# A hybrid backbone block: score products and gate broadcasts over 128 rows instead of 64

## The chip, the core and the metric

The kernel runs as one program on one core of a Trainium2 chip. The metric is the device time of an execution, in microseconds (us). The engines are named as the profile names them: PE (TensorE, matrix products; its weight loads are shown as PEld), DVE (VectorE), ACT (ScalarE), POOL (GpSimd) and SP (SyncE, which here only issues transfers). PE's work is a stream of pairs, a weight load and a product; a product takes a stationary operand of up to 128 rows by 128 columns and streams the columns of a moving operand past it. The profile writes the shape of the array that a product uses as rows*columns: 128*128, or 64*128 where the operands have 64 rows.

## The reference

Two layers work on 256 latent and 256 context tokens of 1024 features; every layer is a feed-forward, a mixer and a second feed-forward. The change touches only the mixer of the first (even) layer, which runs two kinds of heads side by side, four of each:

```python
# differential attention: two score maps of 64 features a head
s = einsum('bqhcd,bkhcd->bhcqk', q, k) * 64 ** -0.5
p = softmax(s)
w = p[:, :, 0] - lam * p[:, :, 1]
out = einsum('bhqk,bkhe->bqhe', w, v)
...
# mLSTM, both directions; 64 features in queries and keys, 128 in values
bcum = cumsum(lf)
dmat = where(tril, bcum[t] - bcum[s] + ig[s], -inf)
s = einsum('bhtd,bhsd->bhts', qc, kc) * exp(dmat - m_t)
h = (einsum('bhts,bhse->bhte', s, vc) + ...) / max(abs(den), exp(-m_t))
...
y = concat([rms_norm(attn), rms_norm(mem) * sigmoid(o_pre)]) @ w_out
```

Context queries see the 256 context keys, latent queries all 512.

## The kernel before

All streams are kept with features on partitions. For precision every float32 operand of a product is split into a high and a low part (float32r), and a product of two such operands is three products: high·high, high·low and low·high (lines 146 to 148 for the projections, 632 to 634 where tokens are on partitions). Weights are loaded raw by SP into a ring of three tiles; ACT casts the high part (line 120), DVE makes the low part (line 121).

The even mixer (`even_mixer`) starts with the projections of the mLSTM queries and keys (`mq`), then the gates: DVE computes cumulative sums and running maxima, and `ga`, 64 rows that hold the gate values of both directions, is split into `gah` (ACT) and `gal` (DVE). `decay_exps(h)` needs one row of `ga`, with all tokens, on all 128 partitions: a product with a one-hot column of `oneh` as the stationary operand, broadcast to 128 columns, does that, once over `gah` (line 799) and once over `gal` (line 800), for both directions of each mLSTM head.

`stack` prepares the score operands of a pair of halves A (partitions 0 to 63) and B (64 to 127), the features of two mLSTM heads or of the two maps of an attention head. For each half there is a 128-row tile of queries, [high, low], and one of keys, [high, high]; the low parts of the keys of both halves share one tile `kl`, half A's in its upper rows and half B's in its lower ones. The tuple `e` says which engine does each of the five steps; the last, the keys' low part (line 843), is POOL's in all six stacks. `score` (lines 849 and 850) then makes a 128-query block of scores of two products into one PSUM bank: the 128-row one, and one of queries' high parts with keys' low parts over the 64 rows of the half. A head has three units: both context blocks (256 keys each), then each latent block (512 keys). So an mLSTM head makes two pairs of products with 256 columns and two with 512, and an attention head (two maps) four and four: 24 pairs of each width in all.

After the scores of a unit come ACT's exponentials, DVE's sums, normalization and combination of two maps or directions (lines 865 to 878, 954 to 970), PE's transposes of the weights (line 890), ACT's copy out (line 892), the products with the values (line 903), the rms norm of the output (`rms_rows`, line 909) and the transposes back (line 912). Between them stand the big projections `ps_v` and `ps_fm`, which fill PE while the other engines work: `qk_pair` (queries and keys of two attention heads, copied out by ACT on line 933 into `qk`), `rows_pair`, `opre_pair`, and the output projection `ps_y`.

The order on each engine is set by a scheduler over the whole program; waits and buffers come from tiles: a tile of a pool has a tag, and tiles of the same tag share its slots, the later one waiting until the earlier one's last reader is done. Projections go to two PSUM banks (`mm_bank`), mLSTM heads to three (`bank_m`), attention heads to three (`bank_a`). The eight `qk` tiles have buffers of their own and are made ahead of the attention; the tiles of a stack are taken from slots of other tiles that are free by then (`slots1`), as the lists at the calls of `stack` and `stack_a` say.

Of the kernel before, what the change touches and what calls it, by code (L numbers as in the profile page):

```python
# [17 lines left out]
P = 128  # L18
# [16 lines left out]
def backbone_kernel(  # L35
# [96 lines left out]
    def split_spare(r3, m, new):  # L132
        """the same into four tiles of half the rows each, where a phase has room for them"""
# [100 lines left out]
    def gemm_first(tiles, bank):  # L234
        """first output tiles of a phase: the norm of the latents between the products of the context"""
# [44 lines left out]
    def norm_steps(l, n, i, sl, bank):  # L280
        """a norm in steps: the tokens' factors, then each chunk of features"""
# [19 lines left out]
    def out_pass(pairs, streams, units, acts, bank, gate, nxt, between=()):  # L301
        """units: (k0, nk, loader) of the rows that a pair of output tiles needs."""
# [273 lines left out]
            # the vectors that come later  # L576
# [10 lines left out]
            # lam[:, 3]: minus the attention's lambda  # L587
# [20 lines left out]
    def proj_first(w, c0, emits, bank, sbank, spare):  # L608
        """c0: columns of the two pairs of tiles; sbank: for the norm's sums"""
# [32 lines left out]
    def rms_rows(src, n, pool, tag):  # L642
        """[tokens, n heads or blocks, features] -> 1 / rms over the features, in columns"""
# [8 lines left out]
        # one Newton step  # L652
# [6 lines left out]
    def out_weights(w, m0, spares):  # L659
        """four output tiles' weights; spares: new tiles for those that spares names, None for the usual ones"""  # L660
# [19 lines left out]
    def even_mixer(nxt):  # L680
# [31 lines left out]
        # mLSTM queries and keys  # L712
# [228 lines left out]
        def stack_a(h, slots):  # L941
            stacks[h] = stack(qk[h], qk[4 + h], slots1(*slots), (nc.vector.tensor_copy, nc.vector.tensor_copy, nc.scalar.copy, nc.vector, nc.gpsimd))
# [505 lines left out]
```

## Time and profile before

| | us |
|---|---|
| median of 3 runs | 1822.99 |
| lowest and highest | 1822.88 and 1828.3 |
| span of the profiled execution | 1823.0 |
| PE busy in it | 1786.7 (98%) |
| DVE, ACT, POOL busy in it | 1153.7, 737.6, 123.1 |
| mean granted TensorE clock | 0.994 |

The span of the profiled execution is its time from the first to the last instruction; it is the median of the runs within 0.01 us. Of the span some 200 us, from about 457 to 652 us, are the heads of the even mixer. PE's busy time counts the modelled length of every product, and products overlap; how fast PE goes is read from the distance between the starts of successive products.

### The profile page before, as it was taken

Reading aid. Unit: us, or ns where it says so; the run is one execution under the profiler, and the core shown is the slowest. Engines: PE = TensorE matmul, PEld = TensorE weight load, DVE = VectorE, ACT = ScalarE, POOL = GpSimd, SP = SyncE. Lnnn points to the kernel's source line nnn. Section 1 sums busy time; section 2 is a strip of 40 time slices with the busy share of each in tenths; the row PEclk is TensorE's granted clock in tenths of the full one; section 3 lists DMA queues with packets and bytes.
Section 4 is the critical chain, followed back from the end, with each engine's and each line's share of the span. In section 5 each row is a group of like instructions: output and inputs, shape, how many; then the busy total and the mean of one; then the engine's idle time right before and its main releaser. Section 6 shows DMA issues by size and latency. Waiting matters only on the chain.

```text
span 1823.0 us, 24907 instructions
## 1 busy us (share of the span) xinstructions
PE 1786.7 (98%) x10095; PEld 1509.5 (83%) x10095; DVE 1153.7 (63%) x1671; ACT 737.6 (40%) x1274; POOL 123.1 (7%) x174
## 2 busy tenths in 40 slices
PE   7999999998999999999999999999999999999998
PEld 5777778898787789777788898777788998889996
DVE  5767776557657857677753476777552747955555
ACT  4322222245656755222222262222222555654443
POOL 1000000014000102000000020000000200010000
PEclk9999999999999999999999999999999999999999
DMA  9555545543121123455543354555432533236553
GB/s 299 168 184 185 184 161 180 165 136 100 48 70 47 47 93 103 155 179 180 181 167 110 104 179 162 164 183 185 162 127 93 182 109 93 70 102 194 191 196 115
DMA packets 209303, 262.29 MB, mean 144 GB/s; under 512 B 6864, under 2 KB 188663, under 8 KB 209189
## 3 DMA queue, kind: packets, MB, share of 16 engines
q1 hardware_dynamic: 208160, 259.28, 43.6%
q8 instruction: 79, 1.29, 0.3%
q0 software_dynamic: 576, 0.84, 0.2%
q10 hardware_dynamic: 452, 0.59, 0.1%
q14 instruction: 36, 0.29, 0.0%
HBM read 259.64 MB, written 1.05 MB: 143 GB/s over the span
## 4 chain that ended last, share of the span: by engine, by line
PE 87%; DVE 7%; ACT 3%; issue 2%; DMA 1%; POOL 1%; SPq 0%; POOLq 0%; ACTq 0%; DVEq 0%
PE ps_ab L146 16%; PE ps_ab L147 16%; PE ps_ab L148 16%; PE ps_y L146 7%; PE ps_y L148 7%; PE ps_y L147 7%; PE ps_fm L146 2%; PE ps_fm L147 2%; PE ps_fm L148 2%; DVE wlo L121 1%; PE po L903 1%; PE ada_ps L190 1%; PE ps_l L1378 1%; PE ps_l L1379 1%; PE ps_v L632 1%
## 5 line engine op out<-in xcount | busy, mean ns | idle before, releaser
L120 ACT CAST whi<-raw 128x1024 fp32r<-128x1024 f32 (+1 forms) x326 | 335.9, 1031 | 847.4 <-PE ps_ab L147 489.8
L121 DVE TENSOR_TENSOR wlo<-raw,whi 128x1024 fp32r<-128x1024 f32 (+1 forms) x326 | 393.1, 1206 | 317.6 <-ACT whi L120 311.2
L146 PE MATMUL ps_ab<-hh,whi 128*128 128x512 f32 (+1 forms) x1360 | 491.0, 362 | 0.8 <-DVE xT L296 0.7
L147 PE MATMUL ps_ab<-hl,whi 128*128 128x512 f32 (+1 forms) x1360 | 490.1, 361 | 1.6 <-POOL hl L275 1.3
L148 PE MATMUL ps_ab<-hh,wlo 128*128 128x512 f32 (+1 forms) x1360 | 489.1, 360 | 0.3 <-DVE wlo L121 0.3
L178 DVE SCALAR_TENSOR_TENSOR acc<-raw_ada,cs,acc 128x1024 f32<-128x1024 f32 x224 | 276.5, 1281 | 41.0 <-DMA raw_ada<-in_ada_w_dram 41.0
L146 PEld LDWEIGHTS ps_ab<-hh,whi 128*128 128x128 f32 x1360 | 255.3, 188 | 49.0 <-ACT whi L120 5.1
L147 PEld LDWEIGHTS ps_ab<-hl,whi 128*128 128x128 f32 x1360 | 255.7, 188 | 45.2 <-POOL hl L275 1.9
L148 PEld LDWEIGHTS ps_ab<-hh,wlo 128*128 128x128 f32 x1360 | 255.6, 188 | 43.5 <-DVE wlo L121 0.5
L148 PE MATMUL ps_y<-gh,wlo 128*128 128x512 f32 (+1 forms) x660 | 229.9, 348 | 0.4
L146 PE MATMUL ps_y<-gh,whi 128*128 128x512 f32 (+1 forms) x660 | 230.0, 348 | 0.0
L147 PE MATMUL ps_y<-gl,whi 128*128 128x512 f32 (+1 forms) x660 | 228.8, 347 | 0.0
L148 PEld LDWEIGHTS ps_y<-gh,wlo 128*128 128x128 f32 x660 | 124.9, 189 | 17.7 <-DVE wlo L121 1.6
L146 PEld LDWEIGHTS ps_y<-gh,whi 128*128 128x128 f32 x660 | 124.9, 189 | 17.2 <-ACT whi L120 1.2
L349 DVE TENSOR_TENSOR s<-ps_ab,s 128x512 f32<-128x512 f32 (+1 forms) x88 | 54.8, 624 | 131.8 <-PE ps_ab L148 130.7
L147 PEld LDWEIGHTS ps_y<-gl,whi 128*128 128x128 f32 x660 | 124.9, 189 | 15.5
L257 POOL TENSOR_TENSOR ssum<-ssum,sq 128x256 f32<-128x256 f32 x33 | 36.2, 1098 | 1133.8 <-ACT sq L255 1133.0
L146 PE MATMUL ps_fm<-hh,whi 128*128 128x256 f32 (+1 forms) x256 | 85.4, 334 | 0.0
L148 PE MATMUL ps_fm<-hh,wlo 128*128 128x256 f32 (+1 forms) x256 | 85.2, 333 | 0.1
L147 PE MATMUL ps_fm<-hl,whi 128*128 128x256 f32 (+1 forms) x256 | 85.3, 333 | 0.0
L633 PE MATMUL ps_v<-wlo,hh 128*128 128x256 f32 x256 | 74.4, 291 | 3.4 <-DVE wlo L121 3.4
L632 PE MATMUL ps_v<-whi,hh 128*128 128x256 f32 x256 | 74.0, 289 | 0.7 <-ACT mv L636 0.7
(377 smaller groups left out, 2395.1 us busy)
## 6 DMA issues: line engine op xcount, KB each, us to landing
raw<-in_ffn_w_in_dram SPq DMA_DIRECT2D x84, 1024.0 KB, 5.3
raw_ada<-in_ada_w_dram SPq DMA_DIRECT2D x64, 1024.0 KB, 5.0
raw<-in_ffn_w_out_dram SPq DMA_DIRECT2D x41, 1024.0 KB, 5.0
raw<-in_even_w_in_dram SPq DMA_DIRECT2D x12, 1024.0 KB, 5.4
raw<-in_odd_w_in_dram SPq DMA_DIRECT2D x12, 1024.0 KB, 5.5
raw<-in_ffn_w_out_dram SPq DMA_DIRECT2D x15, 768.0 KB, 4.2
raw_c<-in_ada_w_dram SPq DMA_DIRECT2D x16, 512.0 KB, 7.6
raw<-in_even_w_out_dram SPq DMA_DIRECT2D x4, 1024.0 KB, 5.5
```

The source lines that it names most:

```text
L120: nc.scalar.copy(hi3, r3)
L121: eng.tensor_tensor(lo3, r3, hi3.bitcast(F32), ALU.subtract)
L146: nc.tensor.matmul(ps, lhsT=wh, rhs=ah, start=first, stop=False)
L147: nc.tensor.matmul(ps, lhsT=wh, rhs=al, start=False, stop=False)
L148: nc.tensor.matmul(ps, lhsT=wl, rhs=ah, start=False, stop=last)
L178: nc.vector.scalar_tensor_tensor(ada_acc[i], r3[:, k2], s, ada_acc[i], ALU.mult, ALU.add)
L190: nc.tensor.matmul(ps[32 * j : 32 * j + 32, :256], lhsT=unit_e[:, 2 * (n - first) + i], rhs=acc[i][:, j * 256 : j * 256 + 256], start=n == ...
L257: (nc.gpsimd if i else nc.vector).tensor_tensor(ssum[i][0], ssum[i][0], sq, ALU.add)
L349: nc.vector.tensor_tensor(s[:, sl], ps[1][:, sl], s[:, sl], ALU.mult)
L632: nc.tensor.matmul(o, lhsT=ah, rhs=wh[:, k4], start=k == 0 and t % 2 == 0, stop=False)
L633: nc.tensor.matmul(o, lhsT=ah, rhs=wl[:, k4], start=False, stop=False)
L903: nc.tensor.matmul(po[:, t], lhsT=w[:, kt, (t % 2) * P : (t % 2) * P + P], rhs=v[:, kt, h * P : h * P + P], start=kt == 0, stop=kt == nk - 1,)
```

## The change

Two places are changed, and the slots of some tiles with them. The comments are dropped too, and lines move by two or three: line 801 after is 799 and 800 before, 840 is new, 846 is 843, 852 and 853 are 849 and 850.

The gates' low parts go into rows 64 to 127 of the tile whose rows 0 to 63 hold the high parts (`gahl`), and `oneh` has the same one-hot columns in both halves. One product over 128 rows then sums both parts, where there were two over 64 rows.

Each half gets a tile of low parts of its own, `kl0` and `kl1`. Its other 64 rows are set to zero by POOL, and the second score product takes the whole query tile and the whole of that tile, 128 rows: the queries' low parts meet zeros.

```diff
-        gah = mp_.tile([P, TT], F32R, tag="gah", name="gah")[0:H2]
-        gal = mp_.tile([P, TT], F32R, tag="gal", name="gal")[0:H2]
-        oneh = mp_.tile([H2, H2], F32R, name="oneh")
-        nc.vector.tensor_copy(oneh, ident[0:H2, 0:H2])
+        gahl = mp_.tile([P, TT], F32R, tag="gah", name="gahl")
+        gah, gal = gahl[0:H2], gahl[H2:P]
+        oneh = mp_.tile([P, H2], F32R, name="oneh")
+        for r in (slice(0, H2), slice(H2, P)):
+            nc.vector.tensor_copy(oneh[r], ident[r, r])
...
-                sel = oneh[:, 32 * d + h : 32 * d + h + 1].to_broadcast([H2, P])
-                nc.tensor.matmul(pA, lhsT=sel, rhs=gah, start=True, stop=False)
-                nc.tensor.matmul(pA, lhsT=sel, rhs=gal, start=False, stop=True)
+                sel = oneh[:, 32 * d + h : 32 * d + h + 1].to_broadcast([P, P])
+                nc.tensor.matmul(pA, lhsT=sel, rhs=gahl, start=True, stop=True)
...
-            (q0, q1, kk0, kk1, kl) = tl
+            (q0, q1, kk0, kk1, kl0, kl1) = tl
             A, B = slice(0, 64), slice(64, P)
-            for qq, kk, s, o in ((q0, kk0, A, B), (q1, kk1, B, A)):
+            for kl, o in ((kl0, B), (kl1, A)):
+                nc.gpsimd.memset(kl[o].bitcast(F32), 0.0)
+            for qq, kk, kl, s, o in ((q0, kk0, kl0, A, B), (q1, kk1, kl1, B, A)):
...
-            return (q0, kk0, kl, A), (q1, kk1, kl, B)
+            return (q0, kk0, kl0), (q1, kk1, kl1)
...
-            nc.tensor.matmul(ps, lhsT=q[s, tk], rhs=kl[s, :n], start=False, stop=True)
+            nc.tensor.matmul(ps, lhsT=q[:, tk], rhs=kl[:, :n], start=False, stop=True)
...
-        qk = [mp_.tile([P, TT], F32, name=f"qk{t}") for t in range(8)]
+        qk = lazy(lambda t: mp_.tile([P, TT], F32, tag=f"qk{t}", name=f"qk{t}"))
...
-        mstk = [stack(mq[0], mq[2], half2 + slots1(("wTa2", 1)), ...
+        mstk = [stack(mq[0], mq[2], half2 + slots1(("wTa2", 1), ("qk2", 1)), ...
...
-        stack_a(0, (("mq1", 1), ("mq3", 1), ("spare", 1), ("th", 2), ("th", 2)))
+        stack_a(0, (("mq1", 1), ("mq3", 1), ("spare", 1), ("th", 2), ("th", 2), ("qk6", 1)))
...
-        stack_a(1, (("mq0", 1), ("mq2", 1), ("gah", 1), ("gal", 1), ("E02", 1)))
+        stack_a(1, (("mq0", 1), ("mq2", 1), ("gah", 1), ("gal", 1), ("E02", 1), ("qk7", 1)))
...
-        stack_a(2, (("spare", 1), ("E02", 1), ("E03", 1), ("E12", 1), ("E13", 1)))
-        stack_a(3, (("mq0", 1), ("mq1", 1), ("mq2", 1), ("mq3", 1), ("gah", 1)))
+        stack_a(2, (("spare", 1), ("E02", 1), ("E03", 1), ("E12", 1), ("E13", 1), ("gal", 1)))
+        stack_a(3, (("mq0", 1), ("mq1", 1), ("mq2", 1), ("mq3", 1), ("gah", 1), ("rsm", 1)))
```

The six new tiles take the slots `qk2`, `qk3` (mLSTM heads 0 and 1, 2 and 3), `qk6`, `qk7` (attention heads 0 and 1), `gal` and `rsm` (2 and 3). The `qk` tiles themselves are now made when they are first written, so `qk2`, `qk3`, `qk6` and `qk7` come after the stacks that borrowed their slots.

The scheduler's order changes in the even mixer alone. First PE, at the start of mLSTM head 0: `pmt` are the transposes that end the gates, `pA` the broadcasts of the two directions, `pS` the scores, `ps_v` a projection. Before:

```order
L778 MATMUL pmt_3501<-ident_67,t1_3484 128x128 x4
L799 MATMUL pA_3533<-gah_3479,oneh_3481 128x512
L800 MATMUL pA_3533<-gal_3480,oneh_3481 128x512
L799 MATMUL pA_3551<-gah_3479,oneh_3481 128x512
L800 MATMUL pA_3551<-gal_3480,oneh_3481 128x512
L849 MATMUL pS_3572<-stk2_3521,stk2_3520 128x256
L850 MATMUL pS_3572<-stk_3522,stk2_3520 128x256
```

The same place after:

```order
L780 MATMUL pmt_3501<-ident_67,t1_3484 128x128 x4
L801 MATMUL pA_3528<-gahl_3479,oneh_3480 128x512
L801 MATMUL pA_3545<-gahl_3479,oneh_3480 128x512
L632 MATMUL ps_v_3625<-whi_3678,hh4_100 128x256
L852 MATMUL pS_3565<-stk2_3513,stk2_3512 128x256
L853 MATMUL pS_3565<-stk_3514,stk2_3512 128x256
```

Four broadcast products have become two, and one projection product has moved ahead of the scores.

Second POOL, while the mixer's first projection runs: `gb` are the gates' biases, `E` and `stk` tiles that are zeroed, `ssum` the sums for the norm of the latents, `hl` the normed latents' low parts. Before:

```order
L706 MEMSET gb_3146 128x1
L822 MEMSET E_3538 128x128
L257 TENSOR_TENSOR ssum_2309<-ssum_2309,sq_3119 128x256
L708 DMA gb_3146<-in_mlstm_gate_b_dram 4x1 x4
L822 MEMSET E_3559 128x128
L275 TENSOR_TENSOR hl1_105<-u_3252,hh1_97 128x256
```

The same place after:

```order
L706 MEMSET gb_3146 128x1
L840 MEMSET stk_3515 64x512
L257 TENSOR_TENSOR ssum_2309<-ssum_2309,sq_3119 128x256
L708 DMA gb_3146<-in_mlstm_gate_b_dram 4x1 x4
L823 MEMSET E_3532 128x128
L823 MEMSET E_3552 128x128
L840 MEMSET stk_3879 64x512
L840 MEMSET stk_4171 64x512
L840 MEMSET stk_4172 64x512
L840 MEMSET stk_4664 64x512
L275 TENSOR_TENSOR hl1_105<-u_3252,hh1_97 128x256
```

Five of the twelve new memsets stand here, one of them ahead of the last sum and four ahead of the first low part.

Third ACT, at the end of attention head 1: `pSa` are its last scores, `wT` transposed weights, `qk7` the last tile of the second `qk_pair`, `stk` tiles of attention head 2. Before:

```order
L958 ACTIVATE ea_4837,st_4838<-pSa_4839,st_4838 128x512
L958 ACTIVATE ea_4837,st_4838<-pSa_4840,st_4838 128x512
L841 CAST stk_5007<-qk6_3517 64x512
L892 COPY wT_4749<-pt_4854 128x4x128
L933 COPY qk7_3518<-ps_fm_4973 128x512
```

The same place after:

```order
L961 ACTIVATE ea_4837,st_4838<-pSa_4839,st_4838 128x512
L961 ACTIVATE ea_4837,st_4838<-pSa_4840,st_4838 128x512
L844 CAST stk_5010<-qk6_4965 64x512
L895 COPY wT_4749<-pt_4854 128x4x128
L936 COPY qk7_5001<-ps_fm_4976 128x512
```

The copy into `qk7` keeps its place, and now also waits for the readers of the stack tile that had its slot.

## Rows read from the trace of the kernel before

**Rows 1.** The page's chain of work that ended last, share of the span by engine.

```profile
PE 87%; DVE 7%; ACT 3%; issue 2%; DMA 1%; POOL 1%; SPq 0%; POOLq 0%; ACTq 0%; DVEq 0%
```

**Rows 2.** Busy time of each engine in stretches of the even mixer's heads: PE, PEld, DVE, ACT, POOL busy us (instructions), granted clock, DMA share, GB/s.

```profile
561.00:576.00 15.00, 14.54 (x78) 10.63 (x76) 13.78 (x35) 12.54 (x30) 3.65 (x2) 1.00 0.04 10
576.00:606.00 30.00, 28.79 (x131) 21.17 (x132) 26.45 (x61) 20.29 (x55) 5.64 (x4) 0.94 0.10 33
```

**Rows 3.** Instructions in order of time, PE alone: start us, length us. The first and the last of nine successive 128-row products of 256 columns, and of twelve of 512 columns.

```profile
454.79 0.28 PE L632 MATMUL ps_v<-whi,hh 128*128 128x256 f32 x1
...
455.73 0.28 PE L634 MATMUL ps_v<-whi,hl 128*128 128x256 f32 x1
...
480.93 0.39 PE L146 MATMUL ps_fm<-hh,whi 128*128 128x512 f32 x1
...
483.50 0.40 PE L148 MATMUL ps_fm<-hh,wlo 128*128 128x512 f32 x1
```

**Rows 4.** The same view at a pair of score products of 512 columns that stands alone in a projection (mLSTM head 1).

```profile
489.08 0.40 PE L849 MATMUL pS<-stk,stk 128*128 128x512 f32 x1
489.41 0.49 PE L850 MATMUL pS<-stk,stk 64*128 64x512 f32 x1
489.83 0.50 PE L146 MATMUL ps_fm<-hh,whi 128*128 128x512 f32 x1
490.17 0.39 PE L147 MATMUL ps_fm<-hl,whi 128*128 128x512 f32 x1
490.39 0.39 PE L148 MATMUL ps_fm<-hh,wlo 128*128 128x512 f32 x1
```

**Rows 5.** The same view, the first and the last of six successive score products of 256 columns (attention head 1).

```profile
574.60 0.39 PE L849 MATMUL pSa<-stk 128*128 128x256 f32 x1
...
576.16 0.38 PE L850 MATMUL pSa<-stk 64*128 64x256 f32 x1
```

**Rows 6.** The same view at the gate broadcasts of mLSTM head 1.

```profile
484.52 0.49 PE L799 MATMUL pA<-gah,oneh 64*128 64x512 f32 x1
484.85 0.39 PE L800 MATMUL pA<-gal,oneh 64*128 64x512 f32 x1
485.09 0.39 PE L799 MATMUL pA<-gah,oneh 64*128 64x512 f32 x1
485.32 0.39 PE L800 MATMUL pA<-gal,oneh 64*128 64x512 f32 x1
485.64 0.38 PE L849 MATMUL pS<-stk,stk 128*128 128x256 f32 x1
```

**Rows 7.** The instructions of lines 849 (its weight loads) and 850: duration ns (least, median, greatest), first and last start us, forms.

```profile
L849 PEld LDWEIGHTS pSa<-stk x32: 186/186/192, 546.8 to 649.2; 128*128 128x128 f32 x32
...
L850 PE MATMUL pSa<-stk x32: 377/438/568, 547.2 to 649.8; 64*128 64x256 f32 x16, 64*128 64x512 f32 x16
...
L850 PE MATMUL pS<-stk,stk x16: 379/441/792, 459.1 to 561.4; 64*128 64x256 f32 x8, 64*128 64x512 f32 x8
```

**Rows 8.** Busy time of each engine in a stretch, columns as in group 2; the clock is the column after POOL's.

```profile
552.00:555.00 3.00, 3.00 (x7) 1.62 (x7) 1.60 (x9) 0.03 (x1) 0.00 (x0) 0.50 0.00 0
```

**Rows 9.** Instructions in order of time, PE alone: the first and the last of 14 successive starts from 550 us (the two in the middle are a pair of score products), and of 9 starts from 601 us (all projections of 512 columns).

```profile
550.27 0.79 PE L146 MATMUL ps_fm<-hh,whi 128*128 128x512 f32 x1
...
556.58 0.54 PE L148 MATMUL ps_fm<-hh,wlo 128*128 128x512 f32 x1
...
601.15 0.53 PE L147 MATMUL ps_fm<-hl,whi 128*128 128x512 f32 x1
...
604.46 0.50 PE L146 MATMUL ps_fm<-hh,whi 128*128 128x512 f32 x1
```

**Rows 10.** Instructions in order of time, all engines; in brackets the idle time before and what ended it.

```profile
553.60 0.69 DVE L865 SCALAR_TENSOR_TENSOR E<-pS,E 128x512 f32<-128x512 f32 x1 [1.40 <-PE pS L850]
...
556.86 0.47 DVE L878 SCALAR_TENSOR_TENSOR E<-E,den 128x256 f32<-128x256 f32 x1
...
560.69 0.38 PE L890 MATMUL pt<-ident,E 128*128 128x128 f32 x2
...
570.49 0.63 PE L890 MATMUL pt<-ident,E 128*128 128x128 f32 x4 [0.46 <-DVE st L962]
...
575.96 1.31 DVE L954 TENSOR_REDUCE st<-pSa 128x2 f32<-128x512 f32 x2 [0.82 <-PE pSa L850]
...
598.55 0.38 PE L850 MATMUL pSa<-stk 64*128 64x256 f32 x1 [0.67 <-POOL stk L843]
```

**Rows 11.** The same view: POOL and PE at the start of the even mixer.

```profile
414.18 0.20 POOL L822 MEMSET E<- 128x128 f32 x1
...
415.38 0.70 PE L287 MATMUL ms<-ssum,ones_d 128*128 128x256 f32 x2 [1.17 <-POOL ssum L257]
...
427.31 0.95 POOL L736 MEMSET gwh<- 128x1024 f32 x1 [2.40 <-PE ps_fm L147]
```

**Rows 12.** The same view: two casts of the same shape on DVE; a subtraction on POOL runs from 441.22 to 442.75 us.

```profile
440.72 0.42 DVE L840 CAST stk<-mq 64x512 fp32r<-64x512 f32 x1
...
441.63 1.41 DVE L840 CAST stk<-mq 64x512 fp32r<-64x512 f32 x1
```

**Rows 13.** The same view: the last score product of attention head 1, and the copy of the last projection of the second `qk_pair`.

```profile
592.29 0.50 PE L850 MATMUL pSa<-stk 64*128 64x512 f32 x1
...
597.43 0.59 ACT L933 COPY qk<-ps_fm 128x512 f32<-128x512 f32 x1
```

More of the change, by code (lines that the diff above doesn't have):

```diff
@@ L843, in stack @@
                 e[4].tensor_tensor(kl[s], k[s], kk[s].bitcast(F32), ALU.subtract)
[L844 removed]
+            return (q0, kk0, kl0), (q1, kk1, kl1)
         def score(ps, stk, t, n):
[L847 removed]
+            q, kk, kl = stk
             tk = slice(t * P, t * P + P)
             nc.tensor.matmul(ps, lhsT=q[:, tk], rhs=kk[:, :n], start=True, stop=False)
[L850 removed]
+            nc.tensor.matmul(ps, lhsT=q[:, tk], rhs=kl[:, :n], start=False, stop=True)
         def halves2(tag, bufs):
@@ L924, in mlstm_head @@
             nc.scalar.activation(mo[h], pv(bank_m, wT, mv, h, "m"), AF.Copy, scale=g_ml[:, h : h + 1])
-        qk = [mp_.tile([P, TT], F32, name=f"qk{t}") for t in range(8)]
+        qk = lazy(lambda t: mp_.tile([P, TT], F32, tag=f"qk{t}", name=f"qk{t}"))
         av = mp_.tile([P, 4, 512], F32, name="av")
-        ao = qk[0:4]
+        ao = qk
         swap = [i ^ 16 for i in range(32)]
         def emit_qk(m, ps):
-            nc.scalar.copy(qk[m], ps)
+            nc.scalar.copy(qk(m), ps)
             sh = mp_.tile([P, T], F32, tag="sh", name="sh", bufs=1)
-            xp = qk[m][:, LAT]
+            xp = qk(m)[:, LAT]
             nc.vector.stream_shuffle(sh, xp, swap)
@@ L941, in stack_a @@
         def stack_a(h, slots):
-            stacks[h] = stack(qk[h], qk[4 + h], slots1(*slots), (nc.vector.tensor_copy, nc.vector.tensor_copy, nc.scalar.copy, nc.vector, nc.gpsimd))
+            stacks[h] = stack(qk(h), qk(4 + h), slots1(*slots), (nc.vector.tensor_copy, nc.vector.tensor_copy, nc.scalar.copy, nc.vector, nc.gpsimd))
         def scores_a(h, unit):
@@ L986, in flush_a @@
             if unit[-1] == 3:
-                nc.scalar.activation(ao[h], pv(bank_a, wT, av, h, "a"), AF.Copy, scale=gd)
+                nc.scalar.activation(ao(h), pv(bank_a, wT, av, h, "a"), AF.Copy, scale=gd)
         def emit_gate(m, ps):
@@ L1004, in even_mixer @@
         half2 = [t for _ in range(2) for t in halves2("ea", 2)]
-        mstk = [stack(mq[0], mq[2], half2 + slots1(("wTa2", 1)), (nc.vector.tensor_copy, nc.vector.tensor_copy, nc.vector.tensor_copy, nc.gpsimd, nc.gpsimd))]
+        mstk = [stack(mq[0], mq[2], half2 + slots1(("wTa2", 1), ("qk2", 1)), (nc.vector.tensor_copy, nc.vector.tensor_copy, nc.vector.tensor_copy, nc.gpsimd, nc.gpsimd))]
         mlstm_head(0, lambda: rows_pair(2048, mv))
-        mstk.append(stack(mq[1], mq[3], halves2("wTa4", 1) + slots1(("mq0", 1), ("mq2", 1), ("rsa", 1)), (nc.vector.tensor_copy, nc.vector.tensor_copy, nc.vector.tensor_copy, nc.gpsimd, nc.gpsimd)))
+        mstk.append(stack(mq[1], mq[3], halves2("wTa4", 1) + slots1(("mq0", 1), ("mq2", 1), ("rsa", 1), ("qk3", 1)), (nc.vector.tensor_copy, nc.vector.tensor_copy, nc.vector.tensor_copy, nc.gpsimd, nc.gpsimd)))
         mlstm_head(1, lambda: None)
         qk_pair(0)
-        stack_a(0, (("mq1", 1), ("mq3", 1), ("spare", 1), ("th", 2), ("th", 2)))
+        stack_a(0, (("mq1", 1), ("mq3", 1), ("spare", 1), ("th", 2), ("th", 2), ("qk6", 1)))
         mlstm_head(2, lambda: None)
@@ L1030, in even_mixer @@
         for h in range(3):
-            out_split(h, ao[h], BOTH)
+            out_split(h, ao(h), BOTH)
         slots = [f"E{d}{t}" for d in range(2) for t in (2, 3)] + ["wTm2", "spare", "dg", "dg"]
@@ L1037, in even_mixer @@
             out_mm(ps[t], ws[t], BOTH, (4, 5, 6, 7, 0, 1, 2), True, False)
-        out_split(3, ao[3], BOTH)
+        out_split(3, ao(3), BOTH)
         new = taker(mp_, [f"mq{t}" for t in range(4)] + ["rsm", "th", "th", "wTm2"], ("th",))
```

1 line of the change is left out of this document (removed).

## Prediction

> **What bounds the kernel now.** The first view is the chain of work that ended last: 87% of it is PE [rows 1], so a microsecond off PE's stream is worth one, unless another engine is late there. The change lies within the even mixer's heads, so the second view is the busy time by stretch [rows 2]: PE is full in all of them, but DVE is nearly so from 561 to 606 us (13.78 of 15 and 26.45 of 30 us). The third view is the order of starts on PE, because busy times overlap. A 128-row product of 256 columns starts every 0.1175 us (0.94 over 8 distances) and one of 512 every 0.2336 us (2.57 over 11) [rows 3]. That is PE's pace when nothing disturbs it; the rest is a comparison with it.
>
> **The score products.** A lone pair of 512 columns: from line 849 at 489.08 to the third projection product after it are four distances, 1.31 us [rows 4], against 4 × 0.2336 = 0.93. It costs 0.38 us more than two plain products. The time is lost at the change of height: 128 to 64 rows takes 0.33, 64 to 128 takes 0.42, and the product after that 0.34, then 0.22 again. In a run of pairs of 256 columns, five distances take 1.56 us [rows 5], 0.312 each instead of 0.1175, so 0.39 us a pair. It is not the 64 rows as such: broadcasts of 64 rows that follow one another are 0.24 and 0.23 us apart [rows 6], the pace of full height. Lines 849 and 850 make 24 pairs of each width [rows 7]. With both products at 128 rows there is no change of height left, and I take the plain pace: 24 × 0.38 + 24 × 0.39 = 18.5 us. The query tile as stationary operand of both products and a moving operand half of zeros have no row of their own; their nearest rows are the plain 128-row products.
>
> **The broadcasts.** From the first of the four to the first score are 1.12 us [rows 6]; two plain products take 0.47, so 0.65 a head, 2.6 us for four. Together 21.1 us of PE's stream. The distances at the entry of a group of pairs are not in this, at most 1 us more.
>
> **The clock.** From 552 to 555 us the granted clock is 0.50, the 1.2 GHz level [rows 8]; before it fell, PE had gone through the broadcasts of mLSTM head 3, six pairs of 256 columns and one of 512, by the prices above 1.1 + 12 × 0.31 + 0.8 = 5.6 us with a change of height at nearly every start. From 550.27 to 556.58 thirteen distances took 6.31 us [rows 9]; plain pace is 3.04, the pair among them is counted above and an exit costs 0.1, so 2.8 us are the clock's. From 601.15 eight distances take 3.31 instead of 1.87: 1.4 us, again behind a run of pairs, with a wait in it. Bounds: 0 if the clock falls anyway, 4.2 if it doesn't. I take 4.2, since that group shrinks to about 2.4 us of dense products (four of 512 and twelve of 256).
>
> **What is late next.** PE comes sooner to places where it waits for others. (1) At 560.69 it transposes weights that DVE finished at 557.33 [rows 10]. It would arrive 6.5 us sooner (0.65 + 6 × 0.39 + 2 × 0.38 + 2.8), at 554.2; DVE's own wait for PE of 1.40 us goes, so the weights are there at 555.9: 1.7 us given back. (2) From 561 to 576 DVE is the pace, and PE already waits 0.46 us for it at 570.49 [rows 10]. What the four pairs ahead of that wait save (one of mLSTM head 3, three of attention head 0), 1.5 us, is lost. Behind it four pairs save 1.56, but DVE waited for them only 0.82 [rows 10]: 0.7 lost. (3) At 598.55 PE waits 0.67 us for POOL's low part [rows 10]; the pairs ahead of it save time that POOL doesn't: 0.6. (4) Other such places (transposes right behind DVE's norms) 0 to 1.2: 0.6. Sum 5.1 us; the bounds are 0, and all that the 16 pairs from 561 to 606 save (6.2) plus (1).
>
> **What is added.** Twelve POOL memsets of 512 columns. A 128-column memset takes 0.20 and a 1024-column one 0.95 us [rows 11], so an estimate between them is 0.5. One takes the place of a 0.20 memset ahead of the sum that PE waits 1.17 us for at 415.38 [rows 11]: 0.3 us onto the path. Queued behind it and the next four are POOL's sums, four transfers of the biases and the latents' low parts, about 0.7 us later; PE has context products to do meanwhile, and if that cover is missing it costs those 0.7. The others precede subtractions for later heads. The second copy for `oneh` on DVE stands far ahead of its use: nothing. Where a memset meets a cast on DVE the cast may be held: one of 0.42 us took 1.41 beside a POOL instruction [rows 12]. I take 0, since a memset would have to meet a cast just where DVE is the pace; the bound is five memsets behind 560 us, 2.6 us. The Trainium skill, page "SBUF — State Buffer", section "Who interferes with whom", speaks against the change here: casts in a two-port mode and any GpSimd instruction lock each other out for a whole instruction, so all twelve memsets could hold DVE, by that rule 12 × 0.5 = 6 us of DVE, of which only those from 561 to 606 reach PE.
>
> **Sum.** 21.1 + 4.2 − 5.1 − 0.3 = 19.9 us off. The profiled span is 1823.0, the median of the runs 1822.99, so both give **1803.1 us**.
>
> **Rivals.** *DVE sets the pace.* If nothing that the 16 pairs and the clock save from 561 to 606 comes through (another 5 us beyond (2) and (3)) and memsets hold casts there (2.6), 12.3 us are left: 1810.7. For it: DVE's 40 of 45 us, and its waits for PE there are short. Against: a DVE whose waits go can itself finish almost 5 us sooner.
>
> *Nothing is late.* PE keeps 21.1 + 1 + 4.2 − 0.3 = 26 us: 1797. The wait at 570.49 speaks against.
>
> *It doesn't do what it says.* The distances of 0.31 and 0.33 come with 128-row weight loads that cannot run beside 128-row products, and stay. If a load of 0.186 us [rows 7] stood ahead of every score product, 256 columns would take 0.30 instead of 0.31 and 512 0.42, a gain of about 1 us, and the broadcasts would gain 0.3 a head: 1821. Against it, loads of 128 rows already run under products of 128 rows: at 0.1175 us a start there is no room for a load of 0.186 [rows 3]. This is what the Trainium skill's page "TensorE: Matmul & The Clock Gate", Part 3, "The mechanism", would give: weight loads overlap with products in flight only when the row group differs. The trace disagrees, at 0.1175 us.
>
> *Slower: the borrowed slot.* The copy into `qk7` now waits until attention head 1 has read its stack. The copy frees one of the two banks that the next six projection tiles go through, four of `opre_pair` with 24 products and two of the output with 21: 138 × 0.2336 = 32 us of PE's fill for attention heads 2 and 3. If these stood behind the heads instead of beside them, the time would be 1823 − 20 + 32 = 1835. It decides from the point where the head's last scores come after that projection has ended; now they are at 592.29 and the copy at 597.43 [rows 13], 5 us to spare, and both move together.
>
> **Chances.** Forecast (1797 to 1807) 0.63, DVE's pace (1807 to 1812) 0.21, nothing late or better 0.07, between 1812 and 1817 0.04, doesn't do it 0.03, slower 0.02. A measurement of this kernel tells 0.3%, 5.5 us, from no change. So faster 0.95, same 0.03, slower 0.02. The range of 1796 to 1811 leaves out some 0.14.
>
> **What would show it.** Right: lines 852 and 853 start 0.118 (256) and 0.234 us (512) apart, no start above 0.30 around them; line 801 twice a head at 0.234; full clock through mLSTM head 3's scores; new waits of PE for DVE at the transposes, 1 to 3 us in all, and DVE busy above 90% in what was 561 to 606. Wrong: distances at 853 that stay at 0.3; clock at 0.50 in the heads; PE waiting for POOL's line 846 or for line 936; the phases after the mixer running otherwise than before.

## The result, and the profile after

| | before | after |
|---|---|---|
| median of the runs on one chip, us | 1825.64 (1822.88 to 1830.17) | 1802.79 (1802.26 to 1806.43) |
| span of the profiled execution, us | 1823.0 | 1800.4 |
| PE, DVE, ACT, POOL busy in it, us | 1786.7, 1153.7, 737.6, 123.1 | 1761.2, 1155.4, 736.6, 127.5 |

The ratio after to before is 0.9887, with a 95% interval from 0.9872 to 0.9902: 1.1% faster, some 20 us. 1803.1 us were predicted.

The spans are 22.6 us apart, but not all of that is the change's. The bounds of the stretch that changed are the sum for the latents' norm (line 287) that ends the work ahead of the mixer, the transposes `pmt` that end the gates, and the transposes `pt_o` that end the last attention head. In the order of starts, before and then after:

```profile
457.08 0.63 PE L778 MATMUL pmt<-ident,t 128*128 128x128 f32 x4 [1.07 <-DVE t L775]
...
662.32 0.63 PE L912 MATMUL pt_o<-ident,on 128*128 128x128 f32 x4
```

```profile
456.48 0.60 PE L780 MATMUL pmt<-ident,t 128*128 128x128 f32 x4
...
640.86 0.63 PE L915 MATMUL pt_o<-ident,on 128*128 128x128 f32 x4
```

From the first to the second the heads take 205.24 us before and 184.38 after: 20.9 us less. Line 287 starts for the first time at 396.96 before and 395.44 after; 1.5 us of the 22.6 therefore lie ahead of everything that the change touches: before, the granted clock was 0.50 from 21.0 to 24.4 us, after it was 1.00 there. From there to `pmt` it is 60.12 before and 61.04 after, 0.9 us more, so that the mixer's net gain is 19.9 us. The 1.2 us that are left lie behind the heads: before, PE's clock was down to half for some of 695 to 700 us (granted clock 0.68 there); after, it was 1.00. In the fourteen profiles of this study line 287 starts for the first time between 395.4 and 398.9 us, whatever the kernel, so the two intervals of the mixer (heads, and line 287 to `pmt`) are what the experiments below are read by; the total is only as sharp as its interval.

**The pace.** PE alone in order of starts, after, at a place of the same kind as [rows 6] and [rows 5]: the broadcasts of mLSTM head 3, its first scores, those of attention head 0, and the projection behind them.

```profile
539.14 0.62 PE L801 MATMUL pA<-gahl,oneh 128*128 128x512 f32 x2
539.60 0.28 PE L852 MATMUL pS<-stk,stk 128*128 128x256 f32 x1
539.72 0.28 PE L853 MATMUL pS<-stk,stk 128*128 128x256 f32 x1
...
540.89 0.28 PE L853 MATMUL pSa<-stk 128*128 128x256 f32 x1
541.01 0.39 PE L852 MATMUL pSa<-stk 128*128 128x512 f32 x1
541.24 0.40 PE L853 MATMUL pSa<-stk 128*128 128x512 f32 x1
541.48 0.40 PE L146 MATMUL ps_fm<-hh,whi 128*128 128x512 f32 x1
```

Twelve products of 256 columns start 0.1175 us apart (1.41 from 539.60 to 541.01), those of 512 columns 0.23 to 0.24, the two broadcasts take 0.46 together. This is the plain pace of [rows 3]: nothing is lost at the scores any more. The whole group takes 2.34 us. The loads of line 853 still take 0.19 us, over 128 rows, and run beside the products:

```profile
L853 PEld LDWEIGHTS pSa<-stk x32: 186/188/193, 540.1 to 628.2; 128*128 128x128 f32 x32
L853 PE MATMUL pSa<-stk x32: 276/388/398, 540.2 to 628.4; 128*128 128x256 f32 x16, 128*128 128x512 f32 x16
```

**The clock.** Busy time by stretch, after; the clock is the column after POOL's. Where it was 0.50 [rows 8] and 0.94 [rows 2], it is 1.00:

```profile
552.00:555.00 3.00, 2.11 (x12) 1.33 (x10) 2.89 (x9) 2.37 (x5) 1.66 (x2) 1.00 0.03 9
539.00:542.00 3.00, 3.00 (x22) 2.73 (x21) 2.21 (x6) 2.62 (x7) 0.00 (x0) 1.00 0.00 0
561.00:576.00 15.00, 14.78 (x92) 12.31 (x90) 12.93 (x36) 12.11 (x41) 0.52 (x1) 1.00 0.22 71
576.00:606.00 30.00, 28.56 (x144) 22.39 (x143) 27.31 (x56) 23.53 (x56) 7.96 (x6) 1.00 0.21 71
```

**The waits.** What PE waited for from 457 to 641.5 us, after (total us, times, longest):

```profile
PE pt L893 <- DVE ea L973: 2.2, 2, 1.4
PE pt_o L915 <- DVE on L912: 1.6, 2, 1.3
PE pt L893 <- DVE E L881: 0.7, 2, 0.4
PE po L906 <- ACT ea L961: 0.4, 2, 0.2
PE pSa L853 <- POOL stk L846: 0.4, 1, 0.4
```

They come to 5.3 us. The same view of before, from 457.5 to 663, has 0.7 for POOL's `stk` and 0.5, 0.5 and 0.2 for DVE, 1.9 in all. So 3.4 us of what PE saved came back as waits, most of them for DVE. Of the prediction's signs of being wrong one shows, a wait for POOL's line 846, but at 0.35 us it is shorter than the 0.67 before. DVE is busy for 40.2 of the 45 us from 561 to 606, as before.

### The profile page after: what moved, and what is told of

Same layout as the page of the kernel before. It is cut to its first block, busy times and chain, and to the rows that moved or that the text cites. A ratio compares the mean times of both kernels' runs of the same rounds, so it can differ in the third digit from the quotient of the medians.

```text
span 1800.4 us, 24909 instructions
## 1 busy us (share of the span) xinstructions
PE 1761.2 (98%) x10087; PEld 1500.5 (83%) x10087; DVE 1155.4 (64%) x1672; ACT 736.6 (41%) x1274; POOL 127.5 (7%) x186
## 4 chain that ended last, share of the span: by engine, by line
PE 86%; DVE 7%; ACT 4%; issue 2%; DMA 1%; POOL 1%; SPq 0%; POOLq 0%; ACTq 0%; DVEq 0%
PE ps_ab L146 16%; PE ps_ab L147 16%; PE ps_ab L148 16%; PE ps_y L146 7%; PE ps_y L148 7%; PE ps_y L147 7%; PE ps_fm L148 2%; PE ps_fm L147 2%; PE ps_fm L146 2%; PE po L906 1%; DVE wlo L121 1%; PE ada_ps L190 1%; PE ps_l L1381 1%; PE ps_l L1382 1%; PE ps_l L1380 1%
```

## The experiments

All intervals are from one profiled execution each: "start" from the first line 287 to `pmt`, "heads" from `pmt` to the last `pt_o`. The ratios are to the kernel before on the same chip; a median of one chip is not compared with one of another.

| run | ratio to before (95%) | start, us | heads, us |
|---|---|---|---|
| before | | 60.12 | 205.24 |
| after | 0.9887 (0.9872 to 0.9902) | 61.04 | 184.38 |
| again (the same kernel) | 0.9903 (0.9887 to 0.9919) | 60.74 | 184.51 |
| rows64 | 0.9981 (0.9973 to 0.9990) | 60.77 | 200.13 |
| scores_only | 0.9901 (0.9888 to 0.9913) | 60.10 | 186.58 |
| broadcasts_only | 0.9975 (0.9964 to 0.9985) | 60.42 | 201.28 |
| sorted | 0.9960 (0.9948 to 0.9972) | 60.15 | 196.73 |
| rows96 | 0.9894 (0.9876 to 0.9912) | 62.53 | 184.42 |
| memset2 | 0.9899 (0.9880 to 0.9918) | 60.72 | 184.46 |
| memset_dve | 0.9901 (0.9886 to 0.9915) | 60.46 | 187.25 |
| oneh1 | 0.9899 (0.9884 to 0.9913) | 60.04 | 184.42 |
| casts_act | 0.9903 (0.9887 to 0.9919) | 60.76 | 187.06 |
| oneh1_act | 0.9905 (0.9891 to 0.9918) | 60.34 | 187.04 |
| swap | 0.9904 (0.9887 to 0.9920) | 60.07 | 187.11 |

The theory is the prediction's: PE loses time wherever a product of 64 rows stands next to one of 128. The rivals: order, slots or engines make the difference; any other number of rows costs the same; each 64-row product costs by itself.

### Again

> The changed kernel once more, to stand beside the two others on the same chip. 1802 to 1806; from the gates' transposes to the end of the heads 184.4 us as in its first profile, since what differs between executions of one program lies ahead of 400 us.

The medians of the changed kernel are 1802.79 in its first runs and 1806.24 here (1801.68 to 1807.9); the heads agree within 0.13 us. Single differences under 3 us in the total say nothing; one of 0.3 us in the heads does, as long as the granted clock in them is compared too.

### 64 rows in the changed kernel

```diff
-            return (q0, kk0, kl0), (q1, kk1, kl1)
+            return (q0, kk0, kl0, A), (q1, kk1, kl1, B)
...
-            q, kk, kl = stk
+            q, kk, kl, s = stk
...
-            nc.tensor.matmul(ps, lhsT=q[:, tk], rhs=kl[:, :n], start=False, stop=True)
+            nc.tensor.matmul(ps, lhsT=q[s, tk], rhs=kl[s, :n], start=False, stop=True)
```

> The changed kernel, but the second score product takes only the 64 rows of its half again (queries' high parts, keys' low parts); memsets, slots, broadcasts and the order on every engine stay as in the changed kernel. Theory (the change of height costs 0.38 us a 512-column pair and 0.39 a 256-column pair): 18.5 us come back on PE's stream, less what waits hide, and the clock's 4.2 us come back if the level falls again: 1816 if it doesn't, 1820.5 if it does; line 853 starts 0.31 us (256 columns) after its partner's start. Rival 1 (order and slots made the gain, not the height): 1803. Rival 2 (the products' pace is the same at 64 rows in this order, and only the broadcasts and the clock gained): 1803 to 1806.

The order is the same on all five engines, and the heads are 15.75 us longer. Since the order is the same, the starts of both can be set side by side: the lag of rows64 behind the changed kernel grows by 0.38 to 0.39 us at nearly every pair, by less where transposes follow a pair, and shrinks where the changed kernel waits. It is 3.20 us at `pmt`, 8.91 ahead of the 512-column pair of attention head 0 at 550.31 and 12.52 at 556.72; two pairs of scores in between account for 0.8 of these 3.6, the clock for 2.8. PE alone, and the window:

```profile
549.80 0.58 PE L853 MATMUL pSa<-stk 64*128 64x256 f32 x1
550.31 0.79 PE L852 MATMUL pSa<-stk 128*128 128x512 f32 x1
551.04 0.79 PE L853 MATMUL pSa<-stk 64*128 64x512 f32 x1
```

```profile
550.00:553.00 3.00, 3.00 (x6) 1.71 (x7) 2.12 (x6) 3.00 (x9) 0.00 (x0) 0.50 0.00 0
```

PE waited for nothing there; ten distances of 0.31 us, a change of height in each, stood ahead, and the granted clock fell to its 1.2 GHz level. Where the lag shrinks it does so by 4.5 us in all (the largest, in the changed kernel's time: 1.55 at the transposes at 555.47, 0.99 at 588.42, 0.43 at the products with the values at 566.18, 0.39 at the transposes at 519.13, 0.33 at POOL's low part at 582.24). So 15.75 = scores + 2.8 − 4.5, and the scores' changes of height are 17.5 us, 0.36 a pair. Order, slots and memsets are not the gain: the heads of rows64 are only 1.15 us shorter than those of broadcasts_only (below), which has the same products in the old order.

### Each part alone

Scores_only keeps the old broadcasts, broadcasts_only keeps the old scores (each takes one hunk of the diff shown with the change).

> The changed kernel with the old broadcasts (two products of 64 rows over separate high and low tiles). Theory: 0.65 us a head come back, 2.6 us: 1805.4, and the clock stays at 1.00 in mLSTM head 3's group, since 5.6 us of products with changes of height have shrunk to about 3: if it falls to 0.50 there, 2.8 us more, 1808. Rival (the broadcasts cost nothing that PE's waits don't hide): 1803.

> The kernel before with the new broadcasts alone (one product of 128 rows over the stacked parts). Theory: 0.65 us a head less, 2.6 us: 1820.4, with the granted clock still at 0.50 for some us around mLSTM head 3, since the twelve starts with changes of height remain. Rival 1 (the broadcasts' 64-row products are the ones that bring the clock down): 4.2 us more off, 1816. Rival 2 (nothing): 1823.

The broadcasts alone take 3.96 us off the heads, the scores alone 18.66, both together 20.86. The 3.96 are the 2.6 and the clock's second fall: the projection products that took 3.31 us from 601.15 to 604.46 [rows 9] take 1.96 here, 1.35 less. The 18.66 of the scores alone are too low by some 1.3: the granted clock of scores_only is 0.50 from 461 to 464 us, at its mLSTM head 0, where no other profile of this study has a fall (products of 256 columns start 0.21 us apart there). Busy time of broadcasts_only from 530 and from 576 us, and of scores_only from 530:

```profile
530.00:561.00 31.00, 30.77 (x162) 24.26 (x162) 13.98 (x41) 16.53 (x45) 0.00 (x0) 0.89 0.22 68
576.00:606.00 30.00, 29.67 (x153) 22.26 (x152) 25.85 (x57) 21.29 (x57) 6.30 (x4) 1.00 0.16 52
```

```profile
530.00:561.00 31.00, 29.43 (x192) 25.78 (x191) 18.90 (x55) 20.45 (x54) 3.10 (x3) 1.00 0.22 68
```

The first fall (0.89 over 31 us) stays with the old scores, whatever the broadcasts are; at mLSTM head 3 four 64-row broadcasts ahead of dense scores don't bring it. Whether those of mLSTM head 0, from 459.27 to 460.39, bring scores_only's own fall at 461 is open. The second fall is there in the kernel before and in sorted (0.94 from 576 to 606 us in both), where PE waits 0.67 and 0.68 us for POOL among the 256-column scores of attention head 2 [rows 10] and these stand in one run. It is not there in rows64 and broadcasts_only, where PE's waits among them are under 0.2 us and four projection products part the run in two. Nor is it in scores_only, where the run is whole and the wait 0.69 us, but no height changes. So the wait alone doesn't bring it; whether it takes the wait or the unbroken run beside the changes of height, no run tells.

### Fewer changes of height with the same 64-row products

```diff
-                for cm in range(2):
-                    score(ps[cm][:, a], stacks[h][cm], t, n)
+                tk = slice(t * P, t * P + P)
+                for cm in range(2):
+                    q, kk, kl, s = stacks[h][cm]
+                    nc.tensor.matmul(ps[cm][:, a], lhsT=q[:, tk], rhs=kk[:, :n], start=True, stop=False)
+                for cm in range(2):
+                    q, kk, kl, s = stacks[h][cm]
+                    nc.tensor.matmul(ps[cm][:, a], lhsT=q[s, tk], rhs=kl[s, :n], start=False, stop=True)
```

> The kernel before, but the attention's scores take the 128-row products of both maps first and then the two 64-row ones, so that the 32 pairs have half as many changes of height; all else as before. Theory (the change of height is what costs): half of 16 x 0.38 + 16 x 0.39 = 12.3 us goes, 6.2 us, 1 to 2 of them lost to DVE's pace: 1817 to 1818. Rival 1 (each 64-row product costs by itself, wherever it stands): 1823. Rival 2 (the two 64-row products of different halves also run side by side): 8 x 0.12 + 8 x 0.23 = 2.8 us more off, 1814 to 1815, and the second of them starts well under 0.1 us behind the first.

The heads are 8.5 us shorter than before, more than the theory's 6.2. The scheduler kept the four products together in the units of 256 columns of all heads but attention head 2 and took most of the 512-column ones apart again. PE alone, a group of two quartets that stayed together:

```profile
548.59 0.50 PE L954 MATMUL pSa<-stk 128*128 128x256 f32 x2
549.02 0.39 PE L957 MATMUL pSa<-stk 64*128 64x256 f32 x2
549.34 0.50 PE L954 MATMUL pSa<-stk 128*128 128x256 f32 x2
549.77 0.39 PE L957 MATMUL pSa<-stk 64*128 64x256 f32 x2
```

A quartet takes 0.75 us instead of 4 × 0.31 = 1.25, at plain pace 0.47. The two 64-row products together (x2) are 0.39 long, as long as one of them alone [rows 5], and start 0.004 us apart: they lie in different halves of the rows and run side by side. And the first fall of the clock is gone (1.00 from 530 to 561), by the prediction's reading 2.8 of the 8.5, so some 5.7 are left for the changes of height and for the halves side by side. The quartet's 0.75 would also fit a cost of each 64-row product that two of them share; what rules that out are the 64-row broadcasts, one after the other at 0.23 and 0.24 us a start [rows 6]. The second rival is right as well: halves do run side by side, which the Trainium skill's page "TensorE: Matmul & The Clock Gate", Part 3, "The mechanism", says of tiles in different rows. It doesn't pay here: even sorted, a quartet costs 0.28 more than four plain products of 128 rows.

### 96 rows

```diff
-            return (q0, kk0, kl0), (q1, kk1, kl1)
+            return (q0, kk0, kl0, slice(0, 96)), (q1, kk1, kl1, slice(0, P))
...
-            nc.tensor.matmul(ps, lhsT=q[:, tk], rhs=kl[:, :n], start=False, stop=True)
+            nc.tensor.matmul(ps, lhsT=q[s, tk], rhs=kl[s, :n], start=False, stop=True)
```

> The changed kernel, but the second product of each half A (first mLSTM head of a pair, first map of an attention head) takes rows 0 to 95 instead of 128; the 32 rows left out are zeros of the keys' tile. Half B's stays at 128 rows; same order on every engine. Theory (what costs is the change between the 64-row and the 128-row use of the array, as the profile writes it, not the number of rows): no distance changes, 1803. Rival (any change of the number of rows costs what 128 to 64 does): 12 pairs of each width at 0.38 come back, 9 us, with or without the clock's 2.8, less 2 to 3 us that waits hide: 1809 to 1812.

```profile
544.63 0.28 PE L852 MATMUL pSa<-stk 128*128 128x256 f32 x1
544.75 0.28 PE L853 MATMUL pSa<-stk 96*128 96x256 f32 x1
544.87 0.28 PE L852 MATMUL pSa<-stk 128*128 128x256 f32 x1
```

96 rows between products of 128 cost nothing: 0.12 us a start, heads within 0.04 us of the changed kernel's. (Its start is longer: the granted clock is down for some of the time around 457 us, 0.94 from 400 to 457 and 0.98 from 457 to 530.) It isn't the number of rows that costs, it is 64 beside 128. The Trainium skill's page "TensorEngine Tiling (Array Packing)", "Key Properties", says that a change of tiling mode drains the engine. By that page of the Trainium skill, section "Available Configurations", a mode of two row tiles is one of 64 rows each. The runs agree as far as they show a loss at just that change, 0.36 to 0.39 us for a way there and back; that it is a drain they don't show.

### The memsets

Memset2 does each memset twice; memset_dve puts them on DVE.

```diff
             for kl, o in ((kl0, B), (kl1, A)):
-                nc.gpsimd.memset(kl[o].bitcast(F32), 0.0)
+                nc.vector.memset(kl[o].bitcast(F32), 0.0)
```

> The changed kernel with each of the twelve memsets done twice on POOL. Theory (a memset costs time only where PE waits for POOL behind it): 0.5 us more ahead of the sum at the mixer's start and up to 0.5 at the low part that PE waits for in attention head 2: 1803.3 to 1804. Rival (memsets hold DVE's casts and subtractions, so twelve more take 0.5 us each from DVE, five of them where DVE is the pace): 2.5 to 6 us more, 1805 to 1809.

> The changed kernel with the twelve memsets on DVE instead of POOL. Theory: PE's wait for the sum at the mixer's start goes from 2.0 us back to about 1.2 to 1.7, and the wait of 0.35 us for POOL's low part in attention head 2 goes; five memsets now stand among DVE's work of the attention heads and cost what DVE takes for one wherever PE waits for DVE (two places): within 1 us of the changed kernel, 1802 to 1804. Rival (DVE is the pace all the way from 561 to 606 us, so each memset there lengthens the whole): 1.5 to 2.5 us more, 1804.3 to 1805.3.

Twelve more memsets on POOL leave the heads at 184.46 and the start at 60.72: the second dozen costs PE next to nothing (0.08 us in the heads), where the rule weighed in the prediction had a bound of 6 us. The section of the Trainium skill's page "SBUF — State Buffer" that the prediction names has a second rule: a DVE instruction with two inputs in SBUF contends with a GpSimd instruction that reads SBUF, not with one that only writes. That agrees with the rows. DVE's combination of attention head 0's weights (line 973, two inputs) behind POOL's memset and beside its subtraction (line 846, which reads), after; and in memset_dve, where the subtraction comes earlier, PE's wait behind the same combination:

```profile
553.28 0.52 POOL L840 MEMSET stk<- 64x512 f32 x1 [28.53 <-DVE den L874]
553.36 0.47 DVE L958 TENSOR_SCALAR st<-st 128x2 f32<-128x2 f32 x1
553.86 1.27 POOL L846 TENSOR_TENSOR stk<-qk,stk 64x512 fp32r<-64x512 f32 x1
553.94 1.86 DVE L973 SCALAR_TENSOR_TENSOR ea<-ea,st 128x256 f32<-128x256 f32 x2
555.47 0.44 PE L893 MATMUL pt<-ident,ea 128*128 128x128 f32 x2 [1.36 <-DVE ea L973]
```

```profile
552.86 1.29 POOL L846 TENSOR_TENSOR stk<-qk,stk 64x512 fp32r<-64x512 f32 x1 [28.50 <-DVE den L874]
554.10 0.87 DVE L973 SCALAR_TENSOR_TENSOR ea<-ea,st 128x256 f32<-128x256 f32 x2
554.63 0.44 PE L893 MATMUL pt<-ident,ea 128*128 128x128 f32 x2 [0.21 <-DVE ea L973]
```

1.86 us instead of 0.87, and a wait of 1.36 instead of 0.21. But one of the first dozen memsets is not free. The small DVE instruction of line 958 ahead of the combination ends 0.03 us behind the memset at 553.28 and takes 0.47 us. In rows64, where that memset comes later, it takes 0.15:

```profile
565.87 0.15 DVE L958 TENSOR_SCALAR st<-st 128x2 f32<-128x2 f32 x1
566.00 0.88 DVE L973 SCALAR_TENSOR_TENSOR ea<-ea,st 128x256 f32<-128x256 f32 x2
```

From the start of the small instruction before it (line 966) to the combination it is 0.78 us in the changed kernel and 0.34 in rows64. So this memset holds DVE for 0.44 us and the subtraction stretches the combination by 1.0: together they account for PE's wait of 1.36. As a whole memset_dve's heads are 2.9 us longer: behind 555 us its order is another one, PE waits 2.73 us for DVE at 590.40 and the granted clock falls to 0.50 from 592 to 594.

### The one-hot columns

```diff
-        for r in (slice(0, H2), slice(H2, P)):
-            nc.vector.tensor_copy(oneh[r], ident[r, r])
+        nc.vector.tensor_tensor(oneh, ident[:, 0:H2], ident[:, H2:P], ALU.add)
```

> The changed kernel with the one-hot columns made by one DVE addition of the identity's left and right half instead of two copies. Theory (the second copy, 0.2 us, shifts DVE's subtractions, beside which POOL's select and sum at the mixer's start take 0.27 and up to 0.4 us longer): PE's wait of 2.0 us for the sum becomes 1.3 to 1.7, 0.3 to 0.7 us less: 1802.1 to 1802.5. Rival (the longer select and sum come from the memset alone): 2.0 us as in the changed kernel.

DVE, POOL and PE at the mixer's start, after and then oneh1 (the lines are one less there):

```profile
410.15 0.72 DVE L753 CAST oneh<-ident 64x64 fp32r<-64x64 f32 x2
411.35 0.92 POOL L697 TENSOR_SCALAR_AFFINE_SELECT tri<-tri 128x128 f32<-128x128 f32 x1
412.96 0.51 POOL L840 MEMSET stk<- 64x512 f32 x1
413.45 1.15 POOL L257 TENSOR_TENSOR ssum<-ssum,sq 128x256 f32<-128x256 f32 x1
414.65 0.70 PE L287 MATMUL ms<-ssum,ones_d 128*128 128x256 f32 x2 [1.99 <-POOL ssum L257]
```

```profile
412.78 0.30 DVE L752 TENSOR_TENSOR oneh<-ident 128x64 fp32r<-128x64 f32 x1
413.99 0.64 POOL L697 TENSOR_SCALAR_AFFINE_SELECT tri<-tri 128x128 f32<-128x128 f32 x1
415.31 0.52 POOL L839 MEMSET stk<- 64x512 f32 x1
415.80 0.72 POOL L257 TENSOR_TENSOR ssum<-ssum,sq 128x256 f32<-128x256 f32 x1
416.57 0.70 PE L287 MATMUL ms<-ssum,ones_d 128*128 128x256 f32 x2 [1.27 <-POOL ssum L257]
```

The wait is 1.27 us instead of 1.99, with the memset still in its place. Scores_only, which has the memset and only one copy, waits 1.28. But broadcasts_only, which has both copies and still the old memset of 0.20 us there, waits 1.22, and memset_dve 1.18, against 1.17 before. So it takes both: the longer memset alone costs 0.1 us, the second copy alone 0.05, the two together 0.8. With the second copy POOL's select takes 0.92 us instead of 0.64 (0.93 in broadcasts_only too); only with the memset behind it does the sum come so late that it takes 1.15 instead of 0.72. That it is DVE's subtractions that the two meet is argued from the times.

### Relieving DVE

```diff
-            stacks[h] = stack(qk(h), qk(4 + h), slots1(*slots), (nc.vector.tensor_copy, nc.vector.tensor_copy, nc.scalar.copy, nc.vector, nc.gpsimd))
+            stacks[h] = stack(qk(h), qk(4 + h), slots1(*slots), (nc.vector.tensor_copy, nc.scalar.copy, nc.scalar.copy, nc.vector, nc.gpsimd))
```

> The changed kernel, but the casts of the keys' high parts for the attention's stacks (eight of 64 rows by 512 columns, 0.42 us each on DVE) are made by ACT. Theory (what the change gave back is PE waiting for DVE where DVE is the pace, 1.36 us and 0.84 us at the transposes of the attention's weights): DVE is relieved of 3.4 us, these two waits shrink by 0.4 to 0.8 each, 1 to 1.5 us less from the gates' transposes to the end of the heads than the changed kernel's 184.4. Rival (ACT, busy 12 of 15 and 24 of 30 us from 561 to 606, becomes the late one): the same waits come back with ACT's exponentials or copies as their cause, 184 to 187.

> The version that the runs so far point to: the changed kernel with the one-hot columns made by one addition (0.7 us less at the mixer's start) and the attention's key casts on ACT. Theory: 0.7 less ahead of the heads and 1 to 1.5 less in them, about 2 us under the changed kernel on the same chip. Rival (ACT becomes late): no better than the changed kernel.

The wait of 1.36 us falls to 0.80, as the theory has it; but POOL's memset and subtraction stand elsewhere in this order and the combination takes 0.87 us, so it is not shown that the casts did it. And the heads take 187.06 and 187.04 us, 2.6 more. Neither theory nor rival had the cause: it isn't ACT that is late, it is DVE still, at another place. The longest of PE's waits of casts_act from 576 to 606:

```profile
PE ps_fm L148 <- DVE wlo L121: 1.8, 1, 1.8
```

PE waits 1.8 us for the low part of a weight, and then runs at the lower clock (granted clock 0.51 from 592 to 594 us).

### Two slots exchanged

```diff
-        stack_a(1, (("mq0", 1), ("mq2", 1), ("gah", 1), ("gal", 1), ("E02", 1), ("qk7", 1)))
+        stack_a(1, (("mq0", 1), ("mq2", 1), ("gah", 1), ("E02", 1), ("gal", 1), ("qk7", 1)))
```

> The changed kernel with the one-hot columns made by one addition, and with two slots of attention head 1's stack exchanged: the low parts of its first half take the slot that is free early and its second keys' tile takes E02, so that the memset at 553.28 us, which waits for E02 and shifts POOL's subtraction onto DVE's combination of attention head 0's weights (1.86 us for two instead of 0.87), comes long before. Theory: the combination takes 0.9 us, PE's wait of 1.36 us ahead of these transposes falls below 0.5, and from the gates' transposes to the end of the heads it is 183.4 instead of 184.4, besides the 0.7 at the mixer's start. Rival (the scheduler's order behind 550 us becomes that of the memsets on DVE, with its wait of 2 to 3 us and its fall of the clock near 590): 186 to 187.

```profile
555.72 1.89 DVE L972 SCALAR_TENSOR_TENSOR ea<-ea,st 128x256 f32<-128x256 f32 x2
555.76 1.57 POOL L845 TENSOR_TENSOR stk<-qk,stk 64x512 fp32r<-64x512 f32 x1 [10.85 <-DVE stk L842]
```

(This run has oneh1's addition too.) The memset is gone from there, and its 0.4 us with it: PE waits 0.97 us at these transposes instead of 1.36. But the subtraction, which now waits for a DVE cast, meets the combination again: 1.89 us. So the theory fails in its larger part: the collision with the subtraction doesn't need the memset. The rival holds: 187.11, with a wait of 1.88 us at 592.93 and the granted clock at 0.51 from 593 to 596. No version beats the changed kernel by more than oneh1's 0.7 us at the start, which no total can show: the medians of oneh1 and of the changed kernel come from different chips, and their ratios overlap.

## Why the prediction was right, and where it was not

- **Scores, 18.5 us predicted: 17.5 measured** (rows64). Mechanism and place are right, and full height restores the plain pace as assumed. The term is 1 us too large: 0.39 a pair was read where pairs stand among products of their own width, and beside the short transposes a pair loses 0.3.
- **Broadcasts, 2.6: 2.6**, as 3.96 less the second fall's 1.35. Beside dense scores they are worth 2.2 (186.58 less 184.38), and some 1.3 of that is scores_only's fall of the clock at 461. Against that PE's waits in the heads are 2.9 us in scores_only and 5.3 in the changed kernel.
- **Clock, 4.2 (2.8 and 1.4): 4.2.** The first fall goes with the scores or with half of their changes of height (scores_only, sorted) and stays when the broadcasts alone are changed. The prediction named the right group. The second fall was put down to a run of pairs with a wait in it, and its size is right. Its reason stays open: the fall is gone in the two runs where the wait is short and the run is parted, and in scores_only, where no height changes.
- **Given back, 5.1: 3.4 net** in the list of waits (4.5 against rows64). The four parts were mis-sized. (1) 1.7 for mLSTM head 3's weights: PE no longer waits long for them; it waits 1.36 at attention head 0's, 1.0 for POOL's subtraction and 0.4 for its memset beside DVE. (2) 2.2 from 561 to 576: 0.4. DVE's waits for PE at the scores (2.0 and 1.4 us from 553 to 600 before) went too and DVE finished sooner; the point that was held against the rival of DVE's pace held against this term as well. (3) 0.6 for POOL's low part: 0.35 is the wait that is left, against 0.67 before. (4) 0.6 for other places: 1.3 at `pt_o` of mLSTM head 1 and 0.84 at 588.42 are the greatest.
- **Added, 0.3 at the mixer's start: 0.6 to 0.9** (61.04, 60.74 and 60.77 us of start against 60.12), and by another cause: the memset, costed at 0.3, gives 0.1 by itself, and 0.8 only together with the copy for `oneh`, which was costed at nothing because it stands far ahead of its use. For the memsets on DVE 0 was taken. Memset2 bears that out for twelve more of them, but the changed kernel has the very meeting that was ruled out: at 553.28 a memset holds DVE for 0.44 us just where PE waits for it.
- **Sum, 19.9: 19.9** over the mixer (265.36 us from the first line 287 to the last `pt_o` before, 245.42 after). One microsecond too much for the scores and 0.6 too little for the start are paid for by 1.7 too much given back: that the sum comes out to the tenth is luck, the mechanism behind its three large terms is not. The profiled span of 1800.4 is 2.7 us below the forecast, by the 1.5 and 1.2 us outside the mixer. The median of 1802.79 and the 1806.24 of the same kernel on another chip lie on either side of 1803.1.
- **The rivals.** DVE's pace did not take 5 us more. Weight loads of 128 rows run beside 128-row products, at 0.1175 us a start. The borrowed slot `qk7` costs nothing: the last scores of attention head 1 start at 577.76, the copy at 581.96, and no copy of line 936 waits.

With the change's own numbers in one line, heads: 17.5 + 2.6 + 4.2 − 3.4 = 20.9 us, which is what the two traces differ by there. The four terms come from different runs, so the match is to some 0.5 us. Along the runs it is 3.96 (broadcasts_only) + 1.15 (order, slots and memsets, to rows64) + 15.75 (scores, to the changed kernel).

What stays open: why the second fall of the clock came, why scores_only has one of its own, and why every other order behind 555 us (memset_dve, casts_act, swap) makes the heads 187 us. There the waits and the falls are shown, the reason for the order is not.

## What to carry to other kernels

Read PE's pace from the distances of starts, and compare it with the nearest undisturbed run of the same width: a short contraction between full ones loses its time at the change, and zeros up to full height, where there is room for them, give it back without a cost on PE. Where PE is full, count on the saved time to reach the end less the waits that it meets, and look for these first at the instructions of DVE with two inputs beside POOL's subtractions, and at small ones beside a memset. "Free" extra instructions on engines with slack still move these engines against each other: 0.2 us of copy and 0.3 of memset, which cost 0.05 and 0.1 us alone, cost 0.8 together here. Read the granted clock beside every interval that you compare: a single fall was worth 1.3 to 1.5 us here.

## What the runs showed of the hardware

- A product of 64 rows between products of 128 costs 0.36 to 0.39 us there and back; one of 96 rows costs nothing; two 64-row products of different halves run side by side, 0.39 us for both.
- The granted clock fell to 0.50 while PE waited for nothing, behind ten distances of 0.31 us with a change of height in each (rows64), and did not where the same products started 0.1175 us apart.
- A POOL subtraction, which reads SBUF, stretched a two-input DVE pair from 0.87 to 1.86 and 1.89 us.
- Twelve more POOL memsets, which only write, cost PE 0.1 us in all; but a DVE tensor_scalar of two columns that met a running memset ended 0.03 us behind it, 0.47 us long instead of 0.15.
